# Both products of an MLP as seven half-size products each (Strassen's scheme), with the norm put on the input

## The chip, the cores and the metric

One core of one Trainium2 chip. The metric is device microseconds for one execution of the kernel. The engines are PE (TensorE: matmuls, with PEld loading its stationary operand), DVE (VectorE), ACT (ScalarE), POOL (GpSimd) and SP (SyncE, which issues the DMAs here). Each engine works through its own list of instructions in the order of that list.

## The reference

An encoder block with one layer, 1024 tokens, width 1024, all in float32. A mixer (neighbourhood attention and gated linear attention) adds to h; then comes the part that this case is about:

```python
def rmsnorm(x, g):
    y = xf * lax.rsqrt(jnp.mean(xf * xf, axis=-1, keepdims=True) + EPS)
    return (y * g)

def sqrelu_mlp(h, ln_g, w1, w2):              # w1: 1024 x 4096, w2: 4096 x 1024
    u = rmsnorm(h, ln_g) @ w1
    return jnp.square(jax.nn.relu(u)) @ w2

h = h + hybrid_mixer(...)                     # ends with a product by w_out
h = h + sqrelu_mlp(h, ln_ff_g, w_ff1, w_ff2)
return rmsnorm(h, ln_final_g)
```

## The kernel before

Everything is held transposed: 128 channels on the partitions, tokens along the free axis, in blocks hT[:, d, :] (d = 0 to 7). The tokens are worked in two halves of 512. float32 accuracy comes from splitting each operand x into a high part (a cast to fp32r, on ACT) and a low part (x minus the high part, on DVE or POOL); `product` issues three matmuls for each 128-channel block: high by high, high by low, low by high. Every matmul of PE is kept in program order; the other engines' lists come from a scheduler that starts from program order, with a priority for some groups and an explicit order for others.

The MLP's 4096 hidden channels go in 8 chunks of 512. `ff1` makes a chunk of u: for each of 4 blocks of 128 hidden channels and each token half, 24 matmuls (8 input blocks x 3), then DVE applies relu and the root factor acc, ACT squares and casts, DVE makes the low part. `ff2` multiplies the chunk by its rows of w2 and DVE adds the result to hT. The root of the norm is a factor per token, so the matmuls read the un-normed input (gff * hT, made by `ff_in` while the output projection, the product with w_out, still runs), and acc comes in after the product. The order is ff1(0), and then ff1(c), ff2(c-1) for c = 1 to 7: a chunk's second product runs one whole first product later. `weights` loads a 128x1024 block (512 KB) and splits it.

In the last chunk the second product goes in three token ranges (512, 256, 256); after each, squares (ACT) and sums (DVE) of the final norm run, a matmul with ones (vf) sums over partitions, `rstd_from` makes the root (steps alternating on ACT and DVE), and DVE and POOL scale hT and SP stores it, beside the matmuls of the next range.

Of the kernel before, what the change touches and what calls it, by code (L numbers as in the profile page):

```python
# [18 lines left out]
P = 128  # L19
# [44 lines left out]
def block_kernel(ctx, tc, xT, g_mix, w_in, w_z, rpb, na_mask, gu, gb, g_gla, sel_f, sel_b,  # L64
# [13 lines left out]
    stg = ctx.enter_context(pool("stg", L, 2))  # L78
# [786 lines left out]
    yp = ctx.enter_context(pool("op", R, 2))  # L865
    n2, acc = {0: half(a2, "n2_0")}, {}


    def ff_in(hf, d):
        c = slice(hf * H, (hf + 1) * H)  # L870
        sq = yp.tile([P, H], F32, tag="sq", name="sq2")
        if d == 0:
            acc[hf] = sq = yp.tile([P, H], F32, tag="acc", name=f"acc{hf}")
        S.activation(sq, hT[:, d, c], AF.Square)
        S.activation(n2[hf][:, d, 0, :], hT[:, d, c], AF.Copy, scale=gff[:, d:d + 1])
        if d:
            (V if hf else G).tensor_tensor(acc[hf], acc[hf], sq, op=ALU.add)
        V.scalar_tensor_tensor(n2[hf][:, d, 1, :], hT[:, d, c], gff[:, d:d + 1],
                               n2[hf][:, d, 0, :].bitcast(F32), op0=ALU.mult, op1=ALU.subtract)

    def ff_rstd(hf):
        v = bank("t", f"v2_{hf}")
        PE.matmul(v, ones, acc[hf], start=True, stop=True)
        rstd_from(v, 1.0 / D, yp, "rs", H, "sq", 2, y=acc[hf])
# [20 lines left out]
    n2[1] = half(a1, "n2_1")  # L905
    ff_in(1, 0)
    for d in range(1, NK):
        run(sums(1, d, KO, V if d < 4 else G))
        ff_in(1, d)
        if d == 3:  # L910
            ff_rstd(0)
# [3 lines left out]
    with pool("u", L) as up:  # L915
        nchunk = FF // P // FCH
        us = {}

        def ff1_part(c, j, hf, w):
            s = slice(hf * H, (hf + 1) * H)  # L920
            uh, ul = us[c, j]
            d = bank("mm" if hf else "s", f"u{c}_{j}_{hf}")
            run(product(d, w, lambda k: n2[hf][:, k, 0, :], lambda k: n2[hf][:, k, 1, :]))
            u = up.tile([P, H], F32, tag="u", name="u", bufs=2)
            V.scalar_tensor_tensor(u, d, 0.0, acc[hf], op0=ALU.max, op1=ALU.mult)  # L925
            S.activation(u, u, AF.Square)  # L926
            S.copy(uh[:, s], u)
            V.tensor_tensor(ul[:, s], u, uh[:, s].bitcast(F32), op=ALU.subtract)

        def ff1(c):  # L930
            for j in range(0, FCH, 2):
                ws = []
                for i in (j, j + 1):
                    ws.append(weights(w1[c * FCH + i]))
                    us[c, i] = (up.tile([P, T], F32R, tag="uh", name="uh", bufs=2 * FCH),
                                up.tile([P, T], F32R, tag="ul", name="ul", bufs=2 * FCH))
                if c == j == 0:

                    ff1_part(c, 0, 0, ws[0])
                    ff1_part(c, 1, 0, ws[1])  # L940
                    ff_rstd(1)
                    ff1_part(c, 0, 1, ws[0])
                    ff1_part(c, 1, 1, ws[1])
                else:
                    for i in range(2):
                        for hf in range(2):
                            ff1_part(c, j + i, hf, ws[i])

        def ff2_part(c, s, d, w):
            n = s.stop - s.start  # L950
            o = bank("o" if d % 2 else "t", f"f2_{c}_{d}_{s.start}")
            run(product(o[:, :n], w, lambda k: us[c, k][0][:, s], lambda k: us[c, k][1][:, s],
                        ks=range(FCH), woff=(d % 2) * FCH * P))
            V.tensor_tensor(hT[:, d, s], hT[:, d, s], o[:, :n], op=ALU.add)  # L954

        def ff2(c):
            for dp in range(NK // 2):
                w = weights(w2[c * (NK // 2) + dp])
                for d in (2 * dp, 2 * dp + 1):
                    for hf in range(2):  # L960
                        ff2_part(c, slice(hf * H, (hf + 1) * H), d, w)

        ff1(0)
        for c in range(1, nchunk):
            ff1(c)
            ff2(c - 1)
        wlast = []
        for dp in range(NK // 2):
            wf = stg.tile([P, D], F32, tag="wf", name="wf")
            DMA.dma_start(wf, w2[(nchunk - 1) * (NK // 2) + dp])  # L970
            wh = up.tile([P, T], F32R, tag="uh", name="uh", bufs=2 * FCH)
            wl = up.tile([P, T], F32R, tag="ul", name="ul", bufs=2 * FCH)
            S.copy(wh, wf)
            V.tensor_tensor(wl, wf, wh.bitcast(F32), op=ALU.subtract)
            wlast.append((wh, wl))
        def finish(c0, n, acc, sq):

            c = slice(c0, c0 + n)
            v = bank("mm", f"vf_{c0}")
            PE.matmul(v[:, :n], ones, acc, start=True, stop=False)  # L980
            PE.matmul(v[:, :n], ones, sq, start=False, stop=True)
# [9 lines left out]
        for c0, n in ((0, H), (H, Q), (H + Q, Q)):  # L991
            c = slice(c0, c0 + n)
            acc = up.tile([P, n], F32, tag="acc", name=f"facc{c0}")
            for d in range(NK):
# [9 lines left out]
                if d > 0:  # L1004
                    next(before, None)
# [86 lines left out]
```

## Time and profile before

| | |
|---|---|
| time, median of 3 runs | 1259.61 us (1259.14 to 1260.28) |
| the profiled execution | 1259.73 us, its span 1257.6 us, mean granted PE clock 0.991 |
| busy share of the span | PE 97%, PEld 80%, DVE 55%, ACT 39%, POOL 12% |
| loads of MLP weights | 64 of 512 KB |

Times in the profile are from the start of the span. A tile's name in a row stands for all its buffers: u is the first product's result, f the second's, op the output projection's, n the input of the MLP (before the root), wh and wl the parts of weights. A matmul's own duration (0.39 us at 512 columns) is longer than the distance between starts, since matmuls overlap; the distance is what counts. A share is an average over stages, so the prediction reads the MLP by itself, in the chain of waits and in windows.

### The profile page before, as it was taken

How to read it: one execution, taken by the hardware profiler on the slowest of the kernel's cores; microseconds unless marked ns; L12 is line 12 of the kernel's file. 1: busy time of each engine (PE TensorE's matmuls, PEld its weight loads, DVE VectorE, ACT ScalarE, POOL GpSimd, SP SyncE). 2: the span in 40 equal slices, each digit the busy share in tenths (PEclk: the TensorE clock that was granted, in tenths of full speed). 3: DMA queues.
4: the chain of work that ended last, by engine and by line, in shares of the span. 5: the costliest groups of instructions: out<-in, count | busy, mean ns of one | idle time of the engine just before them, and what ended most of it. 6: DMA issues, size and time to landing. Idle time of an engine off the chain costs nothing.

```text
span 1257.6 us, 15041 instructions
## 1 busy us (share of the span) xinstructions
PE 1220.2 (97%) x5944; PEld 1004.8 (80%) x5944; DVE 696.7 (55%) x1198; ACT 495.9 (39%) x885; POOL 151.6 (12%) x103
## 2 busy tenths in 40 slices
PE   8989989899999999999999999999999999999995
PEld 8867767678778778788888888888888888888885
DVE  8787877677786965843333333333333333333356
ACT  6657546456455755642312212212113113122054
POOL 4311110312123134500000000000000000000003
PEclk9999999999999999999999999999999999999998
DMA  7210110110111153221111111111111111111113
GB/s 226 72 54 27 41 34 18 34 56 30 34 47 34 46 185 101 84 67 51 51 51 51 51 51 41 44 51 51 51 51 51 51 51 40 45 51 51 34 35 134
DMA packets 37301, 72.99 MB, mean 58 GB/s; under 512 B 8976, under 2 KB 20368, under 8 KB 37232
## 3 DMA queue, kind: packets, MB, share of 16 engines
q1 hardware_dynamic: 36656, 71.11, 18.1%
q8 instruction: 47, 0.77, 0.2%
q0 software_dynamic: 432, 0.93, 0.2%
q14 instruction: 22, 0.18, 0.0%
q10 hardware_dynamic: 144, 0.00, 0.0%
HBM read 67.84 MB, written 5.96 MB: 59 GB/s over the span
## 4 chain that ended last, share of the span: by engine, by line
PE 77%; DVE 14%; ACT 5%; issue 1%; DMA 1%; SPq 0%; DVEq 0%; ACTq 0%
PE u L110 28%; PE f L110 26%; PE proj L110 11%; PE op L110 5%; PE sc L110 2%; PE no L110 1%; DVE st L566 1%; PE pt L113 1%; DVE st L563 1%; DVE b L489 1%; DVE b L487 1%; DVE nl L281 1%; DMA xs<-in_xT 1%; PE c L110 1%; DVE asb L558 1%
## 5 line engine op out<-in xcount | busy, mean ns | idle before, releaser
L110 PE MATMUL u<-n,wh 128*128 128x512 f32 x1024 | 315.6, 389 | 0.0
L170 ACT CAST wh<-wf 128x1024 fp32r<-128x1024 f32 (+1 forms) x103 | 106.5, 1034 | 398.2 <-PE f L110 247.2
L110 PEld LDWEIGHTS u<-n,wh 128*128 128x128 f32 x1024 | 192.3, 188 | 40.3 <-issue 0.5
L110 PE MATMUL u<-n,wl 128*128 128x512 f32 x512 | 199.2, 389 | 0.0
L954 DVE TENSOR_TENSOR hT<-hT,f 128x512 f32<-128x512 f32 (+1 forms) x136 | 88.8, 654 | 189.0 <-PE f L110 189.0
L110 PE MATMUL f<-uh,wh 128*128 128x512 f32 x448 | 174.3, 389 | 0.0
L110 PE MATMUL f<-ul,wh 128*128 128x512 f32 x448 | 174.3, 389 | 0.0
L110 PE MATMUL f<-uh,wl 128*128 128x512 f32 x448 | 174.3, 389 | 0.0
L110 PE MATMUL proj<-nh,wh 128*128 128x512 f32 x352 | 150.8, 429 | 0.8 <-DVE qd L252 0.8
L925 DVE SCALAR_TENSOR_TENSOR u<-u,acc 128x512 f32<-128x512 f32 x64 | 44.3, 692 | 174.3 <-PE u L110 174.3
L110 PE MATMUL proj<-nh,wl 128*128 128x512 f32 x352 | 139.6, 396 | 0.0
L110 PE MATMUL proj<-nl,wh 128*128 128x512 f32 x352 | 139.2, 395 | 0.0
L171 POOL TENSOR_TENSOR wl<-wf,wh 128x1024 fp32r<-128x1024 f32 x36 | 88.4, 2456 | 327.1 <-ACT wh L170 303.4
L110 PEld LDWEIGHTS u<-n,wl 128*128 128x128 f32 x512 | 96.1, 188 | 19.9
L110 PEld LDWEIGHTS f<-uh,wl 128*128 128x128 f32 x448 | 84.1, 188 | 17.4
L110 PEld LDWEIGHTS f<-uh,wh 128*128 128x128 f32 x448 | 84.1, 188 | 17.4
L110 PEld LDWEIGHTS f<-ul,wh 128*128 128x128 f32 x448 | 84.1, 188 | 17.4
L986 POOL TENSOR_TENSOR hT<-hT,fy 128x256 f32<-128x256 f32 (+1 forms) x12 | 11.6, 999 | 706.0 <-issue 692.0
L926 ACT ACTIVATE u<-u 128x512 f32<-128x512 f32 x64 | 40.2, 629 | 140.0 <-DVE u L925 140.0
L171 DVE TENSOR_TENSOR wl<-wf,wh 128x1024 fp32r<-128x1024 f32 (+1 forms) x67 | 81.4, 1218 | 10.4 <-ACT wh L170 10.3
L110 PEld LDWEIGHTS proj<-nh,wh 128*128 128x128 f32 x352 | 67.0, 190 | 19.8 <-issue 5.2
L110 PEld LDWEIGHTS proj<-nh,wl 128*128 128x128 f32 x352 | 67.0, 190 | 15.3
(252 smaller groups left out, 1798.8 us busy)
## 6 DMA issues: line engine op xcount, KB each, us to landing
wf<-in_w SPq DMA_DIRECT2D x64, 512.0 KB
wf<-in_w_in SPq DMA_DIRECT2D x22, 512.0 KB
wf<-in_w_out SPq DMA_DIRECT2D x17, 512.0 KB
hT<-in_xT SPq DMA_DIRECT2D x2, 2048.0 KB
xs<-in_xT SPq DMA_DIRECT2D x6, 512.0 KB
out<-hT SPq DMA_DIRECT2D x8, 256.0 KB
rpb<-rpb SPq DMA_DIRECT2D x16, 96.0 KB
bt<-rpb SPq DMA_DIRECT2D x4, 384.0 KB
```

Of the source, the lines that this page charges most:

```text
L110: tc.keep_in_program_order(nc.tensor.matmul(*args, **kw))
L113: tc.keep_in_program_order(nc.tensor.transpose(*args, **kw))
L170: S.copy(wh[:, c], wf[:, c])
L171: (eng or V).tensor_tensor(wl[:, c], wf[:, c], wh[:, c].bitcast(F32), op=ALU.subtract)
L281: V.scalar_tensor_tensor(nl[:, k, sl], xs[:, k, :], gmix[:, k:k + 1], nh[:, k, sl].bitcast(F32), op0=ALU.mult, op1=ALU.subtract)
L487: V.tensor_tensor_scan(b[0:64, c], rsts[0:64, :], m[0:64, :], 0.0, op0=ALU.mult, op1=ALU.add)
L489: V.tensor_tensor_scan(b[64:128, c][:, ::-1], rsts[64:128, ::-1], m[64:128, ::-1], 0.0, op0=ALU.mult, op1=ALU.add)
L558: V.copy_predicated(asb[hf], sel.bitcast(U32).to_broadcast([P, 4, P]), src.rearrange("p (a b) -> p a b", a=4))
L563: V.scalar_tensor_tensor(st[0:64, i + 1, :], st[0:64, i, :], dec[0:64, i:i + 1], st[0:64, i + 1, :], op0=ALU.mult, op1=ALU.add)
L925: V.scalar_tensor_tensor(u, d, 0.0, acc[hf], op0=ALU.max, op1=ALU.mult)
L926: S.activation(u, u, AF.Square)
L954: V.tensor_tensor(hT[:, d, s], hT[:, d, s], o[:, :n], op=ALU.add)
```

## The change

The MLP's matrices are cut in quarters, and each product is done with seven quarter products instead of eight (Winograd's form of Strassen's scheme). For one chunk and one product:

- Weight quarters A11, A21, A12, A22, 128x1024 each (`Quarters`), are loaded as before, one load per quarter. POOL forms S3 = A11 - A21, S2 = A22 - S3, S1 = A21 + A22, S4 = A12 - S2, four passes of 1024 columns, largely in place. `parts` splits one 512-column half of a quarter or sum into ph and pl (ACT cast, DVE subtraction), three buffers each.
- For the first product the other operand is the normed input: quarters B11, B21 (token half 0) and B12, B22 (token half 1), and T1 = B12 - B11, T3 = B22 - B12, T2 = B11 + T3, T4 = B21 - T2, made once. The root therefore has to be known before the products. Token half 0 is normed and split (n0) while the output projection runs on half 1; what needs half 1 is made after the first three halves of the first chunk's product (T2 as shown in the diff, then T1, T3, B22 and T4 in the same manner, b11, b21 and t2 being sums of parts on POOL).
- For the second product the same sums are made of u in each chunk, by POOL (`Second.prep`), and split into uh and ul (ul on POOL for the first of two hidden blocks, on DVE for the second).
- A quarter product p is two halves of 12 matmuls, one half per hidden block. `First.order` and `Second.order` name the seven. Results that share a product accumulate on in the same PSUM banks; ACT or DVE copies or adds the intermediate states to u, and DVE adds those of the second product to hT.
- `go_on` issues halves and prepares each (cast and low part) two halves ahead, within the list `halves`. The loop puts chunk c's second product directly behind its first: first(c), second(c), first(c+1). The list is extended by second(c) only when first(c) has been issued; first(c+1) is added together with second(c).
- At the end the seventh product of the last chunk goes in two token quarters of 256, with the norm of token half 1 ahead of them and that of each quarter behind it.
- On the host, w1 and w2 are laid out by quarters.

```diff
-    n2, acc = {0: half(a2, "n2_0")}, {}
+    n0, acc = half(a2, "n0"), {}
...
+    def normed_h(dst, hf, d, r):
+        V.scalar_tensor_tensor(dst, hT[:, d, hf * H:(hf + 1) * H], gff[:, d:d + 1], r,
+                               op0=ALU.mult, op1=ALU.mult)
+    def to_two(h, l, x, eng=None, kept=False):
+        c = S.copy(h, x)
+        if kept:
+            tc.keep_in_program_order(c)
+        (eng or V).tensor_tensor(l, x, h.bitcast(F32), op=ALU.subtract)
...
+        if d == 1:
+            r0 = rstd_from(ff_sum(0), 1.0 / D, yp, "rs", H, "sq", 2, y=acc[0])
+            for k in range(NK):
+                nf = yp.tile([P, H], F32, tag="nf", name="nf")
+                normed_h(nf, 0, k, r0)
+                to_two(n0[:, k, 0, :], n0[:, k, 1, :], nf)
...
-        ff1(0)
-        for c in range(1, nchunk):
-            ff1(c)
-            ff2(c - 1)
...
+    KW = {1: "A11", 2: "A12", 3: "S4", 4: "A22", 5: "S1", 6: "S2", 7: "S3"}
+    KB = {1: "B11", 2: "B21", 3: "B22", 4: "T4", 5: "T1", 6: "T2", 7: "T3"}
...
+    class First:
+        order = (1, 2, 6, 5, 7, 3, 4)
...
+        def evac(self, p, g, o):
+            u = self.u
+            if p in (1, 5, 6, 4):
+                k = {1: "B11", 5: "B22", 6: "B12", 4: "B21"}[p]
+                u[k, g] = ub(f"u{k}{g}")
+                if p == 4:
+                    S.activation(u[k, g], o, AF.Relu)
+                    S.activation(u[k, g], u[k, g], AF.Square)
+                else:
+                    S.copy(u[k, g], o)
+            else:
+                t = u[{2: "B11", 7: "B22", 3: "B12"}[p], g]
+                V.tensor_tensor(t, t, o, op=ALU.add)
+                V.scalar_tensor_tensor(t, t, 0.0, t, op0=ALU.max, op1=ALU.mult)
+    class Second:
+        order = (1, 5, 6, 3, 7, 2, 4)
...
+    def go_on(n, ahead=2):
+        for _ in range(n):
+            k = done[0]
+            prep_to(k + 1 + ahead)
+            st, p, i = halves[k]
+            st.mm(p, i, ready[k])
...
+    f1 = First(0)
+    stage(f1)
+    go_on(2, 1)
+    v1 = ff_sum(1)
+    r1 = ub("r1")
+    rstd_from(v1, 1.0 / D, mu, "rs", H, "uh", 3, y=r1)
...
+    for k in range(4):
+        b12[k] = ub("b12") if k < 2 else mu.tile([P, H], F32, tag="uh", name="b12", bufs=3)
+        b22[k] = ub("b22")
+        normed_h(b12[k], 1, k, r1)
+        normed_h(b22[k], 1, k + 4, r1)
+        b11, t3 = temp("b11"), temp("t3")
+        G.tensor_tensor(b11, n0[:, k, 0, :].bitcast(F32), n0[:, k, 1, :].bitcast(F32), op=ALU.add)
+        V.tensor_tensor(t3, b22[k], b12[k], op=ALU.subtract)
+        V.tensor_tensor(t3, t3, b11, op=ALU.add)
+        to_two(*place("T2", k), t3, kept=True)
...
+    for c in range(nchunk):
+        f2 = Second(c, f1.u)
+        go_on(12 if c == 0 else 14)
+        if c + 1 < nchunk:
+            stage(f2)
+            f1 = First(c + 1)
+            stage(f1)
+            go_on(14)
+    stage(f2)
...
+    go_on(10)
+    for k in range(NK):
+        square(H, H, k)
+    go_on(2)
+    finish(H, H, (G, V, G, G))
+    prep_to(k + 2)
+    for c0 in (0, Q):
+        for i in range(2):
+            f2.mm(4, i, ready[k + i], slice(c0, c0 + Q))
+        for d in range(NK):
+            square(c0, Q, d)
+        finish(c0, Q, (V, V, G, V))
```

How this moves instructions is seen in the built programs' lists (line, operation, result, operands, shape; the number behind a name is its buffer). First ACT's list in the middle of the MLP, before, where a first product runs on into the second product of the chunk before it (wh are weights' high parts, u and uh the first product's result and its high part):

```order
L927 CAST uh_7464<-u_7529 128x512
L926 ACTIVATE u_7559<-u_7559 128x512
L927 CAST uh_7472<-u_7559 128x512
L170 CAST wh_7658<-wf_7656 128x1024
L926 ACTIVATE u_7589<-u_7589 128x512
L927 CAST uh_7472<-u_7589 128x512
L170 CAST wh_7720<-wf_7718 128x1024
L170 CAST wh_7782<-wf_7780 128x1024
L170 CAST wh_7844<-wf_7842 128x1024
L170 CAST wh_7852<-wf_7850 128x1024
```

The casts of the second product's weights (from wh_7658 on) wait for no result of the first product beside them. Now ACT's list where a chunk's first product ends and its second begins (ph: high parts of weights; uB210 and uB211: the results of the first product's last two halves; uh: high parts of u):

```order
L891 CAST ph_6539<-A22_5995 128x512
L891 CAST ph_6557<-A22_5995 128x512
L1020 ACTIVATE uB210_6587<-u1_0_6356 128x512
L1021 ACTIVATE uB210_6587<-uB210_6587 128x512
L1020 ACTIVATE uB211_6602<-u1_1_6375 128x512
L1021 ACTIVATE uB211_6602<-uB211_6602 128x512
L891 CAST ph_6613<-A11_6340 128x512
L891 CAST uh_6617<-uB110_6369 128x512
L891 CAST ph_6621<-A11_6340 128x512
L891 CAST uh_6625<-uB111_6388 128x512
L891 CAST ph_6636<-A21_6342 128x512
L891 CAST uh_6640<-T1_6629 128x512
```

The casts for the second product's first half (ph_6613, uh_6617) now stand behind the relu and square of the first product's very last half (uB211). Next POOL, whose list before held, from the output projection's last weights to the final scaling, nothing of the MLP:

```order
L171 TENSOR_TENSOR wl_4808<-wf_4805,wh_4807 128x1024
L171 TENSOR_TENSOR wl_4845<-wf_4842,wh_4844 128x1024
L171 TENSOR_TENSOR wl_4882<-wf_4879,wh_4881 128x1024
L171 TENSOR_TENSOR wl_4919<-wf_4916,wh_4918 128x1024
L986 TENSOR_TENSOR hT_4092<-hT_4092,fy_9086 128x512 x2
L986 TENSOR_TENSOR hT_4092<-hT_4092,fy_9253 128x256 x8
L986 TENSOR_TENSOR hT_4092<-hT_4092,fy_9385 128x256 x2
```

and which now has, at the same transition from a first to a second product, the first product's last weight sum (S2_6349, which becomes S4), the sums of u, the low parts ul, and the second product's weight sums:

```order
L973 TENSOR_TENSOR S2_6349<-A12_5993,S2_6349 128x1024
L1042 TENSOR_TENSOR T1_6629<-uB120_6444,uB110_6369 128x512
L1043 TENSOR_TENSOR uB120_6444<-uB220_6481,uB120_6444 128x512
L894 TENSOR_TENSOR ul_6618<-uB110_6369,uh_6617 128x512
L1046 TENSOR_TENSOR uB110_6369<-uB110_6369,uB120_6444 128x512
L961 TENSOR_TENSOR A11_6340<-A11_6340,A21_6342 128x1024
L964 TENSOR_TENSOR S2_6633<-A22_6346,A11_6340 128x1024
L965 TENSOR_TENSOR A21_6342<-A21_6342,A22_6346 128x1024
L894 TENSOR_TENSOR ul_6641<-T1_6629,uh_6640 128x512
L1042 TENSOR_TENSOR T1_6660<-uB121_6462,uB111_6388 128x512
```

The low part for the first half (ul_6618) and T2 (in place in uB110) stand ahead of the three weight sums of the second product, and these ahead of the low part for its third half (ul_6641). Last, ACT's list at the start of the MLP, before, from the last block of the output projection on (n2_1: input parts of token half 1; rst, rsu, acc1: its root):

```order
L875 ACTIVATE n2_1_4678<-hT_4092,gff_82 128x512
L170 CAST wh_4970<-wf_4968 128x1024
L874 ACTIVATE sq2_4948<-hT_4092 128x512
L875 ACTIVATE n2_1_4678<-hT_4092,gff_82 128x512
L926 ACTIVATE u_5001<-u_5001 128x512
L927 CAST uh_4966<-u_5001 128x512
L926 ACTIVATE u_5031<-u_5031 128x512
L195 ACTIVATE rst_5038<-v2_1_5036,small_91 128x512
L927 CAST uh_4974<-u_5031 128x512
L196 ACTIVATE acc1_4680<-rst_5038,small_91 128x512
L202 ACTIVATE rsu_5041<-v2_1_5036,small_91 128x512
L203 ACTIVATE rst_5038<-acc1_4680 128x512
```

and now, from the end of what is made of token half 1 on (nt holds T2 and T3; ph_5154 is for the fourth half of the first product, ph_5158 for the fifth):

```order
L891 CAST nt_5030<-b12_5056 128x512
L891 CAST nt_5030<-b12_5067 128x512
L891 CAST B22_5032<-b22_5035 128x512
L891 CAST B22_5032<-b22_5046 128x512
L891 CAST B22_5032<-b22_5057 128x512
L891 CAST B22_5032<-b22_5068 128x512
L891 CAST T4_5033<-b21_5118 128x512
L891 CAST T4_5033<-b21_5125 128x512
L891 CAST T4_5033<-b21_5132 128x512
L891 CAST T4_5033<-b21_5139 128x512
L891 CAST ph_5154<-A12_4965 128x512
L891 CAST ph_5158<-S2_4993 128x512
```

The products' casts for token half 1 were made block by block with the projection; now the fourth half's weight cast stands behind all casts of the sums.

More of the change, by code (lines that the diff above doesn't have):

```diff
@@ new lines, in block_kernel @@
+        if d == 1:
[4 more added lines that the diff above has]
+                to_two(n0[:, k, 0, :], n0[:, k, 1, :], nf)
+    yg_pool.close()
+    stg_stack.close()
+    late = lambda name: tc.tile_pool(name=name, bufs=1, side=L, reuse_waits="tile")
+    mu = ctx.enter_context(late("mu"))
+    mw = ctx.enter_context(late("mw"))
@@ new lines, in block_kernel, with stage, prep_to @@
+    halves = []
+    def stage(st):
+        halves.extend((st, p, i) for p in st.order for i in range(2))
+    ready, done = [], [0]
+    def prep_to(n):
+        while len(ready) < min(n, len(halves)):
+            st, p, i = halves[len(ready)]
+            ready.append(st.prep(p, i))
+    def go_on(n, ahead=2):
[4 more added lines that the diff above has]
+            st.mm(p, i, ready[k])
+            ready[k] = None
+            done[0] += 1
```

246 lines of the change are left out of this document (150 added, 96 removed).

## The prediction

> **What bounds the kernel now.** I read the page's shares first, then the chain of waits, then windows, instruction groups by form, and timelines.
>
> ```profile
> span 1257.6 us, 15041 instructions
> PE 1220.2 (97%) x5944; PEld 1004.8 (80%) x5944; DVE 696.7 (55%) x1198; ACT 495.9 (39%) x885; POOL 151.6 (12%) x103
> ```
>
> PE is nearly always busy. The chain, with start, length and what it holds, says that in the MLP it is also what sets the time:
>
> ```profile
> 541.71 10.88 PE u L110 x48
> ...
> 673.18 43.52 PE u L110 x192
> 716.70 43.52 PE f L110 x192
> ```
>
> From 541.71 on the first products (u) and second products (f) follow without a gap: 192 matmuls in 43.52 us, 0.2267 us each. In a middle window the other engines have room (columns: length, then busy us of PE, PEld, DVE, ACT, POOL):
>
> ```profile
> 700.00:800.00 100.00, 100.00 (x443) 82.84 (x442) 36.33 (x46) 22.43 (x31) 0.00 (x0) 1.00 0.15 48
> ```
>
> So fewer matmuls pay in full, as long as PE never waits. Groups by form give the prices of what is added (busy, mean ns):
>
> ```profile
> L926 ACT ACTIVATE u<-u 128x512 f32<-128x512 f32 x64 | 40.2, 629 | 140.0 <-DVE u L925 140.0
> L927 ACT CAST uh<-u 128x512 fp32r<-128x512 f32 x64 | 39.8, 622 | 2.0
> L436 ACT COPY vtok<-vt 128x512 f32<-128x512 f32 x8 | 4.6, 580 | 2.6 <-PE vt L113 2.6
> L954 DVE TENSOR_TENSOR hT<-hT,f 128x512 f32<-128x512 f32 x120 | 82.4, 687 | 186.6 <-PE f L110 186.6
> L928 DVE TENSOR_TENSOR ul<-u,uh 128x512 fp32r<-128x512 f32 x64 | 44.3, 693 | 43.7 <-ACT uh L927 43.7
> L878 DVE SCALAR_TENSOR_TENSOR n<-hT,gff,n 128x512 fp32r<-128x512 f32 x16 | 18.2, 1163 | 0.0
> L171 POOL TENSOR_TENSOR wl<-wf,wh 128x1024 fp32r<-128x1024 f32 x36 | 88.4, 2456 | 327.1 <-ACT wh L170 303.4 <-DVE lm L486 20.0 <-DMA wf<-in_w_out 3.6
> L394 POOL TENSOR_TENSOR qap<-qt,qap 64x512 fp32r<-64x512 f32 x4 | 5.1, 1285 | 14.1 <-ACT qap L390 14.0
> ```
>
> A 512-column pass takes 0.62 on ACT (0.58 out of PSUM), 0.69 on DVE and 1.28 on POOL, whose 1024-column pass takes 2.46 on average and, in the first row below, 2.40. In a row DVE passes start 0.61 apart (second row below: seven in 4.26). DVE and POOL also hinder each other (timelines: start, length):
>
> ```profile
> 521.88 2.40 POOL L171 TENSOR_TENSOR wl<-wf,wh 128x1024 fp32r<-128x1024 f32 x1 [5.44 <-ACT wh L170]
> ...
> 498.44 4.26 DVE L680 TENSOR_TENSOR hT<-hT,opl 128x512 f32<-128x512 f32 x7
> ...
> 503.28 8.55 POOL L877 TENSOR_TENSOR acc<-acc,sq 128x512 f32<-128x512 f32 x5 [0.74 <-ACT sq L874]
> 503.78 6.90 DVE L878 SCALAR_TENSOR_TENSOR n<-hT,gff,n 128x512 fp32r<-128x512 f32 x4
> 513.63 2.82 POOL L171 TENSOR_TENSOR wl<-wf,wh 128x1024 fp32r<-128x1024 f32 x1 [1.80 <-ACT wh L170]
> 519.45 0.74 DVE L878 SCALAR_TENSOR_TENSOR n<-hT,gff,n 128x512 fp32r<-128x512 f32 x1
> ```
>
> The DVE instruction that takes 0.74 with POOL idle (last row) takes 6.90 / 4 = 1.72 beside it, and POOL's 1.28 becomes 8.55 / 5 = 1.71: they take turns, and a DVE turn adds 1.72 - 1.28 = 0.44 to POOL's chain. The adds out of PSUM (0.69) show no such stretch. Most of what the change adds to DVE, and all that it adds to POOL, reads two operands from SBUF, as these rows do.
>
> The Trainium skill ("SBUF — State Buffer", Who interferes with whom) says that a DVE instruction with two SBUF inputs and a POOL instruction that reads SBUF exclude each other for the whole instruction. The alternation agrees, the price less so: whole exclusion would make a pair 0.74 + 1.28 = 2.02, not 1.72; by the rule the sum below would be some 14 us more.
>
> **The change, part by part.** Call a product's half (12 matmuls, 2.72 us) a half, and the 14 halves of a chunk's first or second product stage F or S; there are 8 of each.
>
> Removed on ACT and DVE: the squares, casts and low parts of u per output block and the scaling by the root; none of them is on the chain, so they give nothing.
>
> Matmuls: 168 per stage for 192. 16 x 24 x 0.2267 = -87.0 us. Loads of 512 KB stay 64; the fourth quarter's buffer frees about 6 us before an S begins and is read 8 us into it. I cost it at nothing; the DMA share of 0.15 in the window covers it.
>
> F to S, the main loss. Before, the second product of chunk c-1 ran after the first of chunk c, so its inputs were 43.52 us old. Now S(c) follows F(c) at once, and nothing of S is prepared ahead, since the list of halves ends with F(c) when F(c) is issued. ACT's order there has the evacuation of F's last half (uB211, which waits for F's last matmul, at time E) ahead of the casts that S's first half needs. What follows is worked by each engine's order and the prices above. From E: evacuation 0.58 + square 0.63 + two casts 1.24 = 2.45, first matmul; POOL's low part 1.28, so the second matmul starts at 3.73. PE lost 3.73 - 0.23 = 3.5. Two halves then end at 3.73 + 23 x 0.2267 = 8.95. The third needs S1 of the weights and T1, and POOL has them in line behind that low part: 3.73 + turn 0.44 + T2 1.28 + turn 0.44 + S3, S2, S1 3 x 2.40 = 13.1, casts 14.3, low part 15.6. Lost 15.6 - 0.23 - 8.95 = 6.4. The fourth half waits for T1 of its block (POOL, then cast, then DVE behind T3): 1.0 more; the seventh for S4 and a low part: 0.7. Together 11.6 per chunk. Below: without turns 3.5 + 5.5 = 9.0. Above: POOL at the 2.82 and 1.71 of the rows gives 15.2. I take 11.6, as most rows stand near 2.40: 8 x 11.6 = +92.8. The end of S hides its preparation: there a half has 5.44 us of lead, and DVE's 49 instructions x 0.69 = 33.8 fit into the stage.
>
> F(0), the second loss. Its casts stand behind the last sum of the output projection: add 0.69, square 0.63, cast 0.62, less overlap, then DVE's low part: +2.3. Then PE runs three halves and one sum matmul, and its fourth half's casts stand on ACT and DVE behind all that builds T2, T1, T3, B22, T4 from the second token half. With the last projection matmul at 0, the third half ends at 11.3 (2.7 + 5.0 + 0.86 + 2.72). The root (four ACT, four DVE steps of 0.6 to 0.7 behind the sum at 8.6) lets DVE begin at 13.6. Eighteen DVE passes, 0.63 apart (between the 0.61 in a row and 0.69), and two POOL turns of 1.28: 27.5. Then 20 POOL passes x 1.28 = 25.6, 14 DVE turns x 0.44 = 6.2, and about 2 where POOL's last sums wait for DVE's buffers: 61.3. DVE subtraction and two casts: 62.9. Lost 62.9 - 11.3 = 51.6, taken +52. Without turns 43, with every turn and each wait 56.
>
> Output projection: 16 DVE passes (1.16 each, many beside POOL) go and 16 come, but the root of token half 0 and its 8 casts now stand ahead of the casts of projection weights on ACT. One or two weights come one POOL pass late: 0 to 4.9, taken +3.
>
> Clock. The granted clock dropped once in this trace, near the start:
>
> ```profile
> 8.36 0.38 PE L110 MATMUL z<-nh,wz 128*128 128x256 f32 x1 [1.50 <-ACT nh L280]
> ...
> 11.43 0.41 PE L110 MATMUL sb<-nl,wh 128*128 128x256 f32 x1
> 11.64 0.41 PE L110 MATMUL sb<-nh,wl 128*128 128x256 f32 x1
> ...
> 13.57 0.28 PE L110 MATMUL sb<-nh,wh 128*128 128x256 f32 x1
> 13.69 0.28 PE L110 MATMUL sb<-nl,wh 128*128 128x256 f32 x1
> ```
>
> Behind an idle of 1.5 us (in brackets), starts lie 0.21 apart until about 13.2 instead of 0.12: 3.3 us at half rate, a loss of 1.4. Behind the 6.4 us gap of each S the next wait swallows 1.0 of that: 8 x 0.4, and 1.8 for F(0) and the end: +5, from 0 to +25.
>
> The end (the second, third and fourth row are of the chain, the others of timelines):
>
> ```profile
> 1244.41 0.28 PE L110 MATMUL f<-uh,ul 128*128 128x256 f32 x1
> 1247.43 0.48 ACT ft L195
> ...
> 1249.97 0.42 DVE hT L986
> ...
> 1251.26 1.87 DVE hT L986 x4
> ...
> 1226.27 3.57 POOL L986 TENSOR_TENSOR hT<-hT,fy 128x512 f32<-128x512 f32 x2 [692.05 <-issue]
> 1228.61 1.51 DVE L1002 TENSOR_TENSOR facc<-facc,fsq 128x256 f32<-128x256 f32 x1
> 1249.97 3.15 DVE L986 TENSOR_TENSOR hT<-hT,fy 128x256 f32<-128x256 f32 x6
> ```
>
> Before, the last 24 matmuls (5.44) and the 12.9 from 1244.69 to the span's end: 18.3. In it a root takes 1249.97 - 1247.43 = 2.54, and from the last scaling at 1253.1 to the end, the store, it is 4.5. Now, counted from the last matmul of the sixth product: the seventh's casts stand on ACT behind squares of the finished token half, and a low part on POOL follows, 3.8; 24 matmuls of 256 columns x 0.12, 6.7. The finished half's root is ready at about 8.5; from there POOL scales six 128x512 blocks at 3.57 / 2 = 1.79 beside DVE, to 19, and DVE's seven sums of the first quarter end with them (1.51 for one in such company). Sum matmul 0.6 and root 2.54, six scalings 3.15: 25.4. Only behind these stand the second quarter's adds and sums on DVE, 10 passes of 256 columns at some 0.36, 3.6; then sum and root 3.1, scalings 3.15, store 4.5: 39.7. The old chain also held 5.8 of sums inside (1244.69 - 541.71 less 3072 x 0.2267 and 0.86). 39.7 - 18.3 - 5.8 = +15.6, from +10 to +22.
>
> Sum: -87.0 + 92.8 + 52 + 2.3 + 3 + 5 + 15.6 = +83.7. The profiled execution took 1259.73 (span 1257.6), 0.01% from the median of 1259.61: 1259.7 + 83.7 = 1343.4.
>
> **The rivals.**
> Covered transitions (the other side). If S's first inputs were ready, the 92.8 and 3.2 of clock would go: 1247. The window speaks for it, 78% of ACT idle; against it, ACT and POOL issue in order, and the evacuation ahead can't start before E. It decides below 83.7 / 8, so at a wait under 1.1 per chunk. Chance 0.03.
> No turns. DVE and POOL run side by side: 8 x 9.0 = 72, F(0) 43, end -4: 1309. The 6.90 row speaks against it. Chance 0.09.
> Clock paid each time. Both gaps of each S, 3.5 and 6.4, cost 1.4 and nothing swallows it: 8 x 2.8 + 2 = 24 for 5: 1362. The early rows, where 1.5 us sufficed, speak for it; that the next half waits for POOL anyway against it. The Trainium skill ("TensorE: Matmul & The Clock Gate", What's actually happening) has half rate after an idle window of about 3.4 us and full rate after as much busy time; the 3.3 us agree, the 1.5 us idle does not. Chance 0.12.
> S bound by DVE throughout. If each of its 21 two-input passes waits half a POOL pass, 33.8 + 13 = 47 for 38.1: the last 8 halves stretch by 23%, 5.0 per chunk, +40: 1383. Few POOL passes are left there, which speaks against it. Chance 0.07.
>
> **How the numbers follow.** My forecast, at 0.67, has 1343 with its bounds on the F-to-S wait alone between 1322 and 1372. With 0.09, 0.12, 0.07 and 0.03 for the rivals 0.02 is left for smaller waits all round. From 1305 to 1375 lie the forecast, the no-turns case and the clock case, less the ends of each: about 8 in 10. A change of under 0.2% can't be told from none here. Faster: 0.03; same: 0.01; slower: 0.96.
>
> **What would show it.** In the profile after, PE's row of slices has dips of 7 or less all through the MLP, DVE near 6 and POOL at 5 to 8 there. Matmuls f and u still lie 0.2267 apart inside a half. PE's waits have POOL's low parts and ACT's casts at each F to S, 3 to 4 and 6 to 7 us long, and one of some 50 us near 555 that ends with an ACT cast or DVE's low part. The kernel's last matmuls stand in two groups with over 10 us between. I am wrong if the gaps at F to S are under 2 us, if the one gap is under 35, or if F stages, which I have at 38.1, hold waits of their own.

## The result, and the profile after

The changed kernel takes 1355.3 us (median of 4 runs, 1353.49 to 1358.54) against 1259.47 in the runs beside it: ratio 1.0763, 95% interval 1.0741 to 1.0784. Slower by 96 us, where 1343 and a range of 1305 to 1375 were forecast. The profiled execution took 1353.49, its span is 1351.7.

In the changed kernel L891 is the cast of `to_two`, L894 its low part, L961, L964 and L965 the weight sums S3, S2 and S1, L1046 the sum T2, L1020 and L1021 relu and square of F's last product, L1070 the addition to hT, L1164 the sums of the closing norm. From the page, busy shares and slices:

```profile
PE 1182.7 (87%) x5482; PEld 957.0 (71%) x5482; DVE 949.1 (70%) x1519; ACT 592.2 (44%) x1121; POOL 521.4 (39%) x309
...
PE   9989998999999998409898997998979979989781
...
DVE  8787787678768658664674855857648558485596
...
POOL 3211102221221344381643536427345365263533
PEclk9999999899999999759899898998999989989896
```

PE does 462 matmuls fewer and has holes: one deep one (the 4 and 0), then a 7 or 8 in each chunk; the granted clock dips beside them. What PE waited for (total us, times, longest):

```profile
PE u L111 <- ACT ph L891: 54.9, 2, 52.8
PE f L111 <- ACT uh L891: 44.5, 16, 3.4
PE vf L111 <- DVE fsq L1164: 21.8, 3, 11.7
PE f L111 <- POOL ul L894: 11.5, 16, 0.9
```

Sixteen waits each for casts and POOL low parts are two per chunk. The chain of waits through one turn from F to S and into the next F (start, length):

```profile
908.13 0.61 ACT uB L1020
...
909.89 0.53 ACT uh L891
...
910.49 1.27 POOL ul L894
...
911.85 0.52 POOL uB L1046
...
913.41 2.82 POOL A L961
...
916.31 2.40 POOL S L964
918.71 2.31 POOL A L965
...
921.56 0.62 ACT uh L891
...
922.25 1.29 POOL ul L894
...
923.58 35.16 PE f L111 x143
958.74 38.09 PE u L111 x168
```

F ends at E = 908.11. The second matmul of S follows the low part, at E + 3.7; the third half waits for T2 and three weight sums, one behind the other on POOL, and its second matmul starts at E + 15.47. The next F is 168 x 0.2267 = 38.09 long: no wait in it. F starts lie 88.74 apart where 2 x 38.09 = 76.18 would do, so S loses 12.56 a chunk. The rows of PE's timeline (in brackets the idle ahead and what ended it) show how:

```profile
910.47 0.51 PE L111 MATMUL f<-uh,ph 128*128 128x512 f32 x1 [2.38 <-ACT uh L891]
911.82 0.79 PE L111 MATMUL f<-ul,ph 128*128 128x512 f32 x1 [0.85 <-POOL ul L894]
...
922.23 0.80 PE L111 MATMUL f<-uh,ph 128*128 128x512 f32 x1 [3.35 <-ACT uh L891]
923.58 0.80 PE L111 MATMUL f<-ul,ph 128*128 128x512 f32 x1 [0.56 <-POOL ul L894]
924.17 0.63 PE L111 MATMUL f<-uh,pl 128*128 128x512 f32 x1
924.60 0.63 PE L111 MATMUL f<-uh,ph 128*128 128x512 f32 x1
...
929.11 0.40 PE L111 MATMUL f<-uh,pl 128*128 128x512 f32 x1
929.34 0.39 PE L111 MATMUL f<-uh,ph 128*128 128x512 f32 x1
```

Behind the second gap starts lie 0.43 apart until 928.9, then 0.23 again. That is all that the 143 matmuls have over 143 x 0.2267 = 32.4: 2.7 us. Behind the first gap the half rate costs some 1.7 us too, but that only shortens the second gap, whose end POOL's chain sets.

The start of the first chunk and the end, from the chain:

```profile
610.38 32.31 PE u L111 x132
...
1311.53 2.08 PE vf L111 x2
...
1328.68 1.24 PE vf L111 x2
...
1340.40 1.24 PE vf L111 x2
```

### The profile page after: what moved, and what is told of

It is laid out like the page before. It is cut to its first block, busy times and chain, and to the rows that moved or that the text cites. A ratio compares the mean times of both kernels' runs of the same rounds, so it can differ in the third digit from the quotient of the medians.

```text
span 1351.7 us, 15223 instructions
## 1 busy us (share of the span) xinstructions
PE 1182.7 (87%) x5482; PEld 957.0 (71%) x5482; DVE 949.1 (70%) x1519; ACT 592.2 (44%) x1121; POOL 521.4 (39%) x309
## 4 chain that ended last, share of the span: by engine, by line
PE 66%; DVE 15%; POOL 9%; ACT 6%; issue 3%; DMA 1%; SPq 0%; DVEq 0%; ACTq 0%; POOLq 0%
PE u L111 23%; PE f L111 20%; PE proj L111 11%; PE op L111 5%; POOL A L961 2%; POOL ul L894 2%; PE sc L111 1%; POOL S L964 1%; POOL A L965 1%; PE no L111 1%; DVE st L567 1%; PE pt L114 1%; DVE st L564 1%; DVE fsq L1164 1%; PE o L111 1%
## 5 line engine op out<-in xcount | busy, mean ns | idle before, releaser
L894 DVE TENSOR_TENSOR pl<-A,ph 128x512 fp32r<-128x512 f32 x160 | 154.8, 969 | 145.5 <-ACT ph L891 144.8
L111 PE MATMUL f<-uh,ph 128*128 128x512 f32 (+1 forms) x456 | 192.9, 423 | 44.5 <-ACT uh L891 44.5
L111 PE MATMUL f<-ul,ph 128*128 128x512 f32 (+1 forms) x456 | 192.6, 422 | 11.5 <-POOL ul L894 11.5
L891 ACT CAST ph<-A 128x512 fp32r<-128x512 f32 x160 | 99.1, 620 | 235.1 <-PE f L111 105.9
L111 PE MATMUL f<-uh,pl 128*128 128x512 f32 (+1 forms) x456 | 189.0, 414 | 0.0
L1070 DVE TENSOR_TENSOR hT<-hT,f 128x512 f32<-128x512 f32 (+1 forms) x228 | 141.1, 667 | 24.7 <-PE f L111 24.7
L111 PEld LDWEIGHTS f<-uh,ph 128*128 128x128 f32 x456 | 95.2, 209 | 71.9 <-ACT uh L891 51.8
L111 PE MATMUL u<-n,ph 128*128 128x512 f32 x256 | 81.1, 398 | 54.9 <-ACT ph L891 54.9
L111 PEld LDWEIGHTS f<-ul,ph 128*128 128x128 f32 x456 | 94.8, 208 | 37.9 <-POOL ul L894 17.9
L894 POOL TENSOR_TENSOR ul<-uB,uh 128x512 fp32r<-128x512 f32 x48 | 66.0, 1376 | 112.9 <-ACT uh L891 108.3
L111 PEld LDWEIGHTS f<-uh,pl 128*128 128x128 f32 x456 | 94.4, 207 | 19.4
L111 PE MATMUL u<-nt,ph 128*128 128x512 f32 x256 | 78.8, 389 | 0.0
L894 DVE TENSOR_TENSOR pl<-S,ph 128x512 fp32r<-128x512 f32 x64 | 60.8, 953 | 24.1 <-ACT ph L891 23.5
```

The source lines that it names most:

```text
L111: tc.keep_in_program_order(nc.tensor.matmul(*args, **kw))
L891: c = S.copy(h, x)
L894: (eng or V).tensor_tensor(l, x, h.bitcast(F32), op=ALU.subtract)
L1070: V.tensor_tensor(hT[:, d, c], hT[:, d, c], o[:, s], op=ALU.add)
```

## The experiments

All ratios are to the kernel before, run on the same chip.

| run | us | ratio, 95% interval |
|---|---|---|
| as changed | 1355.3 | 1.0763, 1.0741 to 1.0784 |
| halves ahead | 1330.9 | 1.0556, 1.0540 to 1.0572 |
| sums in another order | 1328.1 | 1.0542, 1.0524 to 1.0559 |
| both | 1324.8 | 1.0512, 1.0496 to 1.0528 |
| clock kept up | 1349.4 | 1.0709, 1.0693 to 1.0725 |
| building between products | 1342.6 | 1.0658, 1.0641 to 1.0674 |
| end in one range | 1351.7 | 1.0726, 1.0704 to 1.0748 |
| products reordered | 1335.8 | 1.0604, 1.0589 to 1.0620 |
| all so far | 1318.5 | 1.0473, 1.0444 to 1.0502 |
| POOL's order kept | 1326.3 | 1.0527, 1.0508 to 1.0547 |
| that with building and end | 1314.0 | 1.0423, 1.0402 to 1.0443 |
| S without weight sums | 1295.6 | 1.0280, 1.0263 to 1.0297 |
| all, S's sums on DVE | 1291.9 | 1.0253, 1.0238 to 1.0268 |

**Is it the order at the turn?** First the halves ahead:

```diff
-        go_on(12 if c == 0 else 14)
+        go_on(10 if c == 0 else 12)
+        stage(f2)
+        go_on(2)
         if c + 1 < nchunk:
-            stage(f2)
...
-    stage(f2)
```

> In each S stage the first two halves (the product with A11, which needs no weight sum) are prepared before F's last two halves are evacuated, not behind them; nothing else moves. Theory A (the order of the small work at the turn from F to S costs the time): the first gap of 3.67 us between the last matmul of F and S's second one goes, the sums start earlier by the same, so the second matmul of S's third half comes about 12.8 us after F's end instead of 15.5, and S loses some 9 us a chunk instead of 12.6: 1325 us (1320 to 1332). Rival B (DVE and POOL together are too slow for S, so the time returns later in the same stage): 1355 within 4 us.

1330.9, as theory A has it: F starts lie 85.4 apart, so S loses 9.2. The first gap is gone, and the longest wait of the second grew from 3.4 to 5.6. Rival B falls as far as the first gap goes.

Then the sums, without that:

```diff
-            G.tensor_tensor(t["A11"], t["A11"], t["A21"], op=ALU.subtract)   # S3
-            G.tensor_tensor(t["S2"], t["A22"], t["S3"], op=ALU.subtract)
-            G.tensor_tensor(t["A21"], t["A21"], t["A22"], op=ALU.add)        # S1
+            G.tensor_tensor(t["A21"], t["A21"], t["A22"], op=ALU.add)        # S1
...
+            G.tensor_tensor(t["S2"], s1, t["A11"], op=ALU.subtract)
...
+            G.tensor_tensor(t["A11"], t["A22"], s2, op=ALU.subtract)         # S3, when asked for
```

> The weight sums are formed in another order: S1 = A21 + A22, S2 = S1 - A11, S3 = A22 - S2 (the same values), so that the sums that the second product needs no longer wait for the casts of A11; S's first halves stay where they are. Theory A: the first gap stays at 3.7 to 4.5 us, the second (now 7.3 us in all at S's third half) falls to 2 or less, and with no gap of over 3 us there the clock isn't halved after it; S loses about 6 us a chunk, 1303 us (1295 to 1315). Rival B (throughput of DVE and POOL): 1355 within 4 us, the waits at later halves of S.

1328.1, half of what theory A had. POOL's and PE's timelines tell why:

```profile
810.69 2.40 POOL L962 TENSOR_TENSOR A<-A,A 128x1024 f32<-128x1024 f32 x1 [22.47 <-DMA A<-in_w]
...
816.83 1.60 POOL L1053 TENSOR_TENSOR uB<-uB,uB 128x512 f32<-128x512 f32 x1
818.40 1.71 POOL L894 TENSOR_TENSOR ul<-uB,uh 128x512 fp32r<-128x512 f32 x1
820.16 0.79 PE L111 MATMUL f<-ul,ph 128*128 128x512 f32 x1 [3.33 <-POOL ul L894]
```

The second gap is gone, but the first grew. Sums that need nothing of F's cast could start when their weights had landed, and the scheduler put them, and T1 and T3, ahead of the 1.3 us low part that S's second matmul waits for. Both edits together:

> Both of the two edits before: the halves of A11 prepared ahead of F's last evacuation, and the sums in the order S1, S2, S3. Theory A: both gaps at the turn nearly gone, 4 us a chunk left, 1286 us (1278 to 1300). Rival B (throughput of DVE and POOL): 1340 to 1355, with TensorE's waits moved to S's later halves or to F's first ones. Rival C (the two edits' gains are for the same wait): no better than the better of the two alone.

1324.8: rival C, nearly. S loses 8.3 a chunk. Each edit takes a piece from one line of work on POOL, and PE waits for what is then last in it.

**Does the half clock matter?** 22 matmuls more fill part of the second gap:

```diff
+                if p == 5 and i == j == 0:
+                    (ph, _), (qh, _) = self.kept
+                    for _ in range(22):
+                        PE.matmul(o[:, s], ph[:, 0:P], qh[:, s], start=True, stop=True, skip_group_check=True)
```

> 22 more matmuls of the same size, on operands already there and into a bank that the next product overwrites, stand on TensorE between S's second and third half, where it waits 7.3 us in all for the third half's operands. They change no result. Theory A (the operands' readiness bounds, the half clock behind the gap costs 2.75 us less the 1.7 us of later waits that it covers): 1 us a chunk gained, 1347 us (1343 to 1352). Rival C (the half clock is paid in full): 2.75 us a chunk, 1333 us. Rival D (the added matmuls are longer than the gap): up to 1357.

1349.4, 5.9 gained: theory A. Rival D has little room: in the chunk from 868.45 on, the third half's first matmul starts at E + 14.3, against E + 14.1 without the added ones. The granted clock in the third half is 1.00 and the half's matmuls lie 0.23 apart, yet F starts still lie 87.9 apart, since other waits come instead. PE's waits in this run hold a kind that the changed kernel's did not:

```profile
PE f L111 <- ACT uh L891: 19.0, 8, 2.4
PE f L111 <- POOL ul L894: 9.9, 16, 0.9
PE f L111 <- DVE ul L894: 3.0, 6, 0.6
```

**Is the 52.8 us gap an order too?**

```diff
     go_on(2, 1)
+    prep_to(5)
     v1 = ff_sum(1)
     r1 = ub("r1")
+    go_on(2, 1)
...
         to_two(*place("T2", k), t3, kept=True)
+    go_on(2)
...
+    go_on(2)
+    for k in range(4):
+        to_two(*place("T3", k), b12[k], kept=True)
+    go_on(2)
```

T1 and B22 are built ahead of the third of these go_on, T4 behind the fourth, with one more go_on(2) behind it.

> In F of the first chunk the halves of products 2 and 6 are prepared ahead of the building of T2, T1, T3, B22 and T4, and the building stands between the products that need each matrix, not whole ahead of the fourth half. The turns from F to S stay as in the changed kernel. Theory A (the 52.8 us gap is an order: TensorE waits for all five matrices where it needs one): half of the gap is covered by products 2 and 6 and by parts of 5, 7 and 3; some 27 us gained, 1328 us (1318 to 1338). Rival B (the building needs DVE and POOL whole for some 50 us and TensorE's products take as much of them as they cover): under 10 us gained, 1346 to 1355.

1342.6: 12.7 gained, between the two. The page's first row of this run and windows in the gap (length, then busy of PE, PEld, DVE, ACT, POOL; then the granted clock):

```profile
PE 1199.2 (89%) x5482; PEld 962.6 (72%) x5482; DVE 952.7 (71%) x1519; ACT 590.8 (44%) x1121; POOL 523.8 (39%) x309
```

```profile
563.00:580.00 17.00, 4.03 (x6) 1.58 (x6) 16.97 (x20) 1.74 (x3) 7.31 (x4) 0.60 0.09 31
580.00:600.00 20.00, 13.23 (x29) 7.24 (x30) 10.56 (x11) 6.72 (x14) 18.78 (x13) 0.67 0.08 27
```

PE's waits in F(0) fell from 54.9 in all to about 28, but the same 5482 matmuls are busy for 16.5 us more: they came singly behind short gaps, where a matmul overlaps no other, and at 0.6 to 0.7 of the clock. And the building itself is a chain: DVE is busy for 16.97 of the first 17 us, POOL for 18.78 of the next 20. Both parts are shown; how they would divide at full clock was not tried.

**The end in one range.**

```diff
-    for c0 in (0, Q):
-        for i in range(2):
-            f2.mm(4, i, ready[k + i], slice(c0, c0 + Q))
...
-        finish(c0, Q, (V, V, G, V))
+    for i in range(2):
+        f2.mm(4, i, ready[k + i])
...
+    finish(0, H, (V, G, V, V))
```

> The seventh product of the last S takes all 512 tokens at once instead of two ranges of 256, and the closing statistics and scaling follow once. Theory A (the end's 43.4 us are waits in a row for DVE and POOL, and two ranges bring two of them): 10 to 13 us gained, 1343 us (1339 to 1347). Rival B (the first range's closing work lies under the second's, as it was written for): nothing gained or up to 5 us lost, 1355 to 1360.

1351.7: about 3.6 gained, but the intervals of the two ratios just overlap, so that the gain is at the edge of the noise. One wait for the sums of the norm went and PE's total for them fell from 21.8 to 14.3; the work behind it, at 512 columns instead of 256, took most of that back.

**What holds S then?** With both edits of the turn, the products were reordered:

```diff
-        order = (1, 5, 6, 3, 7, 2, 4)
+        order = (1, 2, 5, 6, 7, 3, 4)
```

> As the run with both edits of the turn, and S takes its products in the order 1, 2, 5, 6, 7, 3, 4: the second product (A12 by B21) needs no sum of either side, so four halves stand between F's end and the first sum. In the run with both edits S's third half still waits for one chain on POOL, of three weight sums of 2.8 us each, three token sums and two low parts, some 17 us after F's end. Theory A (order): with 10.9 us of matmuls of the first four halves and the lookahead, most of that chain is covered; 0 to 3 us lost a chunk instead of 8, 1261 to 1285 us, 1272 as the likeliest. Rival B (POOL and DVE throughput in S): no gain on 1325, the same waits at the fifth and later halves.

1335.8, slower than the 1324.8 without it: theory A falls. (In this run and the next the closing norm of token half 1 stands ahead of product 3 of the last chunk, so what they store is not the block's result; the instructions are the same in number.) POOL's and PE's timelines:

```profile
815.58 2.86 POOL L962 TENSOR_TENSOR A<-A,A 128x1024 f32<-128x1024 f32 x1
...
829.03 1.26 POOL L894 TENSOR_TENSOR ul<-uB,uh 128x512 fp32r<-128x512 f32 x1
830.35 0.79 PE L111 MATMUL f<-ul,ph 128*128 128x512 f32 x1 [5.48 <-POOL ul L894]
```

Product 2 needs no sum, but its low part stands on POOL behind S1, S2, S3, T1, T3 and T2, 13.5 us of them. All edits so far:

> All edits together: the turn (halves ahead, sums in the order S1, S2, S3, products 1, 2, 5, 6, 7, 3, 4), the building of F's first matrices between the products, the end in one range. Theory A (all of the loss is order, and the matmuls' 87 us stand): 1272 less 27 and less 12 is 1233 us (1220 to 1250), under the 1260 of the kernel before. Rival B (DVE and POOL bound S, or the building): 1265 to 1300, slower than before.

1318.5: rival B's side, and 18 over its range. So POOL's list was written out, every one of its sums and low parts in the MLP kept in program order, with the sums called for where they are wanted:

```diff
-            G.tensor_tensor(t["A21"], t["A21"], t["A22"], op=ALU.add)
+            pool_tt(t["A21"], t["A21"], t["A22"], op=ALU.add)     # kept in program order
...
+            self.soon = {(1, 1): ("S1", "S2"), (5, 0): ("T11", "T30", "T20"),
+                         (6, 0): ("T31", "T21", "S3"), (7, 0): ("S4",)}
```

> As the run with S's products in the order 1, 2, 5, 6, 7, 3, 4 (the last chunk keeps 1, 5, 6, 3, 7, 2, 4, so that the closing norm of token half 1 stands behind all its products), but POOL's work in the MLP is kept in a written order: S1 and S2 behind the first low part, then the low part of product 2, then T1, its low part, and each further sum just ahead of its use. In the run before, the low part of product 2 (1.26 us) stood on POOL behind S1, S2, S3, T1, T3 and T2 and TensorE waited 5.5 us for it in each chunk, then at half clock. Theory A (what the low part is queued behind on POOL is the wait): that wait and the one after it go, 1 to 4 us a chunk left where there were 10; 1335 less 8 times 7 is 1280 us (1268 to 1292). Rival B (POOL and DVE, which take turns, hold S up by their sum): 1315 to 1335, with waits of 2 to 4 us spread over S's later halves.

1326.3: rival B. (Here, and in the next run, S4 of the last chunk overwrites S2 between the two halves of product 6, so what is stored is not the block's result; the instructions are the same in number.) S's window, and rows of DVE, POOL and PE in it:

```profile
817.50:862.90 45.40, 40.42 (x170) 32.36 (x169) 41.11 (x46) 16.56 (x29) 30.77 (x19) 0.96 0.13 47
```

```profile
817.43 2.74 POOL L949 TENSOR_TENSOR S<-A,A 128x1024 f32<-128x1024 f32 x1
...
817.83 2.90 DVE L894 TENSOR_TENSOR ul<-uB,uh 128x512 fp32r<-128x512 f32 x1
...
824.04 0.68 DVE L894 TENSOR_TENSOR ul<-uB,uh 128x512 fp32r<-128x512 f32 x1
824.64 2.47 DVE L1104 TENSOR_TENSOR hT<-hT,f 128x512 f32<-128x512 f32 x4
...
832.01 0.76 PE L111 MATMUL f<-uh,ph 128*128 128x512 f32 x1 [2.97 <-DVE hT L1104]
...
846.31 0.47 PE L111 MATMUL f<-uh,ph 128*128 128x512 f32 x1 [1.69 <-DVE hT L1104]
```

No long wait for POOL is left, but DVE is busy for 41.1 of 45.4 us, and PE waits for its additions to hT, at the first matmuls of product 5 (832.01) and of product 7 (846.31). A low part that takes 0.68 takes 2.90 where POOL's pass of 2.74 started just ahead of it. F starts lie 83.5 apart, S loses 7.3. That is 2.5 a chunk less than in the run before, but F(0) ended 7 us later (at 647.8 for 640.8). And the time is rival B's without its mechanism being shown: by the code, products 2 and 5 use the same PSUM banks, and so do 6 and 7, and each pair now stands side by side, so that the later of the two waits until DVE has taken what the earlier left there. In the old order no two neighbours share banks, and the run with both edits of the turn has no wait of PE for hT at all. So these waits are of the new order as well as of DVE's turns.

With the edits of building and end as above:

> The run with POOL's order kept, with two edits tried alone before: the building of F's first matrices between the products (12.7 us gained alone), and the end in one range (3.6 us gained alone). Theory A: the three gains add up, 1280 less 16 is 1264 us (1250 to 1276). Rival B (they share POOL and DVE, so the gains overlap): 1275 to 1320. Faster than the kernel before (under 1257) only if S's waits go wholly; a chance of 2 in 10.

1314.0, 12.3 less: most of the 16.3 that these two edits gained alone is there, the gain forecast for POOL's order was not. Is it DVE's turns? From the run with POOL's order kept, for S alone:

```diff
-            if key == "S1":
+            if self.plain:
+                t[key] = t[{"S1": "A21", "S2": "A22", "S3": "A11", "S4": "A12"}[key]]
+            elif key == "S1":
```

> The run with POOL's order kept, and in the second product the four weight sums are left out (the quarters A21, A22, A11 and A12 stand where S1, S2, S3 and S4 were), so POOL does 10.9 us less in each S; DVE's and ACT's passes and TensorE's matmuls are the same in number. In the run before, S took 45.4 us and DVE was busy for 41.1 of them, with low parts at 1.5 us that take 0.69 where POOL is idle. Theory A (DVE bounds S, through the time it waits its turn with POOL): fewer turns, DVE busy about 36 us a stage, the waits for the additions to hT nearly gone, 5 to 6 us a chunk gained, 1280 us (1272 to 1292). Rival B (the time lies in order and buffers, with POOL's sums beside the path): within 8 us of 1326.

1295.6: 30.7 gained, two thirds of what theory A had and far from rival B. The windows of two S, one chunk between them:

```profile
816.67:858.03 41.36, 38.43 (x169) 31.38 (x169) 36.81 (x45) 16.67 (x29) 23.00 (x16) 1.00 0.16 52
896.11:939.08 42.97, 40.04 (x169) 32.51 (x169) 37.00 (x45) 16.56 (x29) 23.08 (x16) 0.96 0.15 50
```

F starts lie 79.4 and 81.0 apart by turns, as these two windows show, the longer with a spell of half clock. The one row of PE's timeline in the first that begins behind a wait (the second has the same wait, at 909.92):

```profile
830.48 0.47 PE L111 MATMUL f<-uh,ph 128*128 128x512 f32 x1 [2.93 <-DVE hT L1107]
```

On average S loses 4.0 a chunk instead of 7.3. POOL is busy for 7.8 us less, DVE for 4.3 less with one pass fewer in the window, and the wait at product 7 is gone: so DVE's turns with POOL's weight sums did cost, though not the 5 to 6 a chunk of theory A. One wait of 2.9 is left, at the first matmul of product 5: the banks that products 2 and 5 share, with nothing between them to cover DVE's four additions. Without POOL's sums it is as long as with them (2.97), so it is a cost of my order of products. Last, every edit, with S's sums on DVE:

```diff
-            self.w, self.u, self.b, self.c = Quarters(w2[c]), u, {}, c
+            self.w, self.u, self.b, self.c = Quarters(w2[c], V.tensor_tensor), u, {}, c
```

> All edits together once more (halves ahead, the sums S1, S2, S3, products 1, 2, 5, 6, 7, 3, 4 but in the last chunk 1, 5, 6, 3, 7, 2, 4, POOL's order kept, F's first matrices built between products, the end in one range), and S's weight sums go from POOL to DVE, four passes of 1024 columns that I estimate at 1.25 us each, twice the 0.62 us between rows of 512. Theory A (DVE with its turns bounds S): DVE gains 5 us of passes and loses about as much in turns, so little changes: 1314 before, 1305 to 1320 now. Rival B (POOL's chain of sums is the wait): 6 us a chunk gained, 1270 to 1290.

1291.9, next to rival B's range and not in theory A's. The window of an S in this run:

```profile
799.21:842.90 43.69, 40.20 (x170) 32.52 (x169) 39.27 (x48) 16.61 (x29) 23.27 (x16) 0.96 0.14 49
```

DVE makes the sums, at 1.2 us each, and is still busy for less in S than with POOL making them (39.3 against 41.1). Over a whole chunk, F and S, with four passes more, it is busy for 63.6 to 64.0 where it was 64.0 to 64.7 in the run with building and end: a sum's turn had cost DVE about what the sum itself costs. So the two were rightly put equal, and what fails in theory A is the step from DVE's busy time to the length of S. S is 1.7 shorter than there, and of its waits the one at product 7 went from 1.6 to 0.5, the one at product 5 stayed at 3.0. This is the fastest of the kernels with seven products, and it is 2.5% slower than the kernel before.

## Why the prediction was right, point by point

- **Matmuls, -87.0.** F stages at 38.09 where 38.1 was forecast; 0.2267 a matmul holds wherever nothing waits.
- **Output projection, +3, and first casts, +2.3.** The projection ends at 545.8, 4.1 later; the casts cost 2.7.
- **F(0), +52.** The wait is 52.8, in the order that was named. Not in the term: 2.4 of half clock in the 132 matmuls behind it (32.31 for 29.9). (The forecast's last steps, a subtraction of 0.69 and two casts of 0.62 behind 61.3, make 63.2 and not 62.9; it is +52 either way.)
- **F to S, 11.6 a chunk.** Second matmul at E + 3.7 (forecast 3.73), third half's second at E + 15.47 (15.6). The waits of the second gap are 3.35 and 0.56 where 6 to 7 was forecast, since the matmuls ahead of it ran 1.7 longer; POOL's chain sets its end, as forecast. The two later waits of 1.0 and 0.7 did not come; in their place stands the half clock, 2.7. So 12.56 for 12.0 with the clock's share; over the chunks 11.7 + 7 x 12.56 = 99.6 for 96. That the half clock and the later waits cover each other, as the forecast had it against the rival, is shown by the run with the clock kept up: 5.9 gained and not 22.
- **Clock, +5.** Of the terms this one was mis-sized the most in proportion: behind the second gap it cost 2.7 a chunk where 0.4 was left of it, as the spell there is 6.8 us long and not 3.3; F(0)'s 2.4 stands against 1.8 for F(0) and the end. Its source was also misread. In the profile before the granted clock dropped not once: it is 0.77 from 134 to 138, 0.74 from 185 to 190, 0.83 from 240 to 250 and lower again behind the last products. And near the start it is 1.00 until 9.8 and 0.50 from 9.9 to 13.2, so the first matmuls behind the idle of 1.5 us still ran at full clock.
- **The end, +15.6.** The last F ends at 1263.1, so the sixth product's matmuls at 1263.1 + 12.56 + 144 x 0.2267 = 1308.3; from there it is 43.4 to the span's end where I had 39.7: +19.3. The last root's matmul runs at 1340.4, where I had it at 39.7 - 3.1 - 3.15 - 4.5 = 29.0 past 1308.3, so 1337.3; most of the miss is there, in sums and scalings of DVE beside POOL.
- **Sum.** -87.0 + 4.1 + 2.7 + 52.8 + 2.4 + 99.6 + 19.3 = 93.9, and 1259.7 + 93.9 = 1353.6, for an execution of 1353.49.
- **The rivals.** No turns: POOL's first weight sum takes 2.82 beside DVE, its second 2.40 without. Covered transitions: the gaps are there. Clock in full: above. S bound by DVE throughout: not in the changed kernel, where DVE is busy for 37.9 of the 50.6 us from E to the next F; with the turn mended DVE's turns with POOL's sums do cost S some 3 a chunk (F starts 83.5 apart with them, 80.2 without). The price of 5 is not confirmed by the 7.3 of the run with POOL's order kept: 4.7 of these are the waits at the two pairs of products that share banks, and 1.7 is half clock.
- **The signs.** The two gaps of each turn, the one of some 50 us, the F stages without waits and the last matmuls in two groups 12 us apart came as named. PE's slices dip to 7 or 8, where 7 or less was named, and POOL stands at 2 to 7 behind the first chunk, where 5 to 8 was.

Of the 100 us that the eight turns cost, the edits of order alone gave back some 30 (both edits of the turn). In the fastest kernel S still loses 5.3 a chunk on average, of which 3.0 is product 5's wait for its banks and, in most chunks, 1.7 the half clock behind it: the new order of products, more than work on DVE and POOL. An order in which no neighbours share banks, with the sums on DVE, was not run. And the largest single piece that is left there lies elsewhere: of the 57.9 that F(0) lost (2.7, 52.8 and 2.4), 47.8 still stand, from the projection's end at 546.7 to S's first matmul at 633.5, less 168 matmuls and the 0.86 of the norm's sum.

## What to carry to other kernels

Fewer matmuls are worth their full price only where what they need is ready: price the sums and splits on the engines that make them, in the stage where they fall, in that engine's order, and with the turns that two engines cost each other. When an edit makes work ready earlier, ask what it now stands ahead of in its queue; three edits here moved the same wait instead of ending it. Before two products stand side by side, ask whether they share banks. Filling a long gap with scattered matmuls gains less than the wait that goes: here some 27 us of wait went and 12.7 were gained.

## What the runs showed of the hardware

The granted clock fell to one half for 3.4 us or a multiple of it, and not at once behind an idle. In the turn shown it is 1.00 until 911.8, 0.50 until 915.2, 1.00 again, and 0.50 from 922.0 to 928.9. In the 3.4 us just ahead of these two spells PE is busy for 0.51 us (908.4 to 911.8) and 0.25 us (918.6 to 922.0). The length of an idle alone does not tell its price: in S without weight sums the same wait of 2.93 us brought one spell of half clock in the chunk at 909.92 and none in the chunk at 830.48. I take it that what counts is how little PE does in such a stretch; no run tried it by itself.

DVE passes with both operands in SBUF wait for POOL's pass to end (2.90 for 0.68, its POOL pass having 2.34 still to run); those with one operand in PSUM do not stretch (2.47 for four; 0.68 on average for the additions to hT in each S that was read). The Trainium skill ("SBUF — State Buffer", Who interferes with whom) says both, and here the rows agree. The prediction weighed the first by a shorter POOL pass, 1.28, where whole exclusion looked too dear; the second it had from its own rows.
